# A hybrid decoder layer on one core: bias strips from a table of ready rows, and a new order of the projections and tasks

## The chip, the cores and the metric

The kernel runs on one core of a Trainium2 chip. A core has five engines that each work through their own list of instructions in order: TensorE (PE, matrix products), VectorE (DVE), ScalarE (ACT), GpSimd (POOL) and SyncE (SP), which here issues nearly all transfers. Engines wait for one another, and for transfers, at semaphores. The metric is the time of one execution on the device in microseconds (us); lower is better.

## The reference

One step of a decoder layer with D = 1024, for a prompt of 512 tokens and 8 sample tokens that continue cached sequences. One input projection gives the inputs of two mixers: gated linear attention with 4 heads (qa, ka, va, a gate of rank 16 called za, and an output gate ga), and dilated sliding-window attention with 8 heads of 64 (qb, kb, vb, gb). The second one matters here. Every query reads its keys at three patterns of distance (up to 128 in steps of 1, up to 512 in steps of 4, up to 2048 in steps of 16), each with a bias that depends on head and distance alone:

```
bias   = rel_bias[t5_bucket(dist)].T                    # one row per head
logits = einsum('bqhd,bqjhd->bhqj', q, k) * scale + bias
p      = exp(logits - m);   s = sum(p)                  # per pattern, merged by their sums
mix    = concat(o_a * silu(ga), o_b * silu(gb))
y      = mix @ w_out;  x_new = layer_norm(alpha * x + y, ln_g, ln_b)
```

All is in float32. Outputs are also the new recurrent states and the key and value rows.

## The kernel before

A float32 product is made as three passes over a high and a low part (`hi` times `hi`, `hi` times `lo`, `lo` times `hi`; helper `three`). The weights arrive as raw tiles (`raw_qb`, `raw_kb`, ...), a group of columns at a time; ACT casts the high part (`hi_kb<-raw_kb`), DVE subtracts to get the low part (`lo_kb`), and PE runs the group's 48 (256 feature columns: two token halves of 24) or 96 matmuls. These "dense" matmuls come in the order of the list `ORDER` (line 79).

All work is recorded by generators, each added as a task with a rank: `add(weight_loads(), 14.7)`, `add(strips(), 2.3)`. A planner (`class Plan`, line 201) simulates engines and transfers with costs of its own and at each moment begins, among what could start, the operation of the best rank; `dense()` has rank 100 and fills PE where nothing else is ready. What comes out is one fixed list of instructions for every engine, and the chip runs those lists whatever its real times are. So a changed rank or cost reorders all engines, SP's transfers too. Every recorded operation is emitted by line 377, so the profile shows that line nearly everywhere and groups must be told apart by tile names.

Transfers on SP go through eight semaphores in turn, so SP issues a transfer only when the one eight places earlier has landed. The order it issues them in is the order in which most of them land.

The bias goes this way. `bias_table()` makes `tsb`, for each of 8 heads a row of 768 values (512 by distance, 128 masked, 128 far ones), stores it to DRAM as `tab`, and a transfer inside DRAM copies it 35 times to `tabr` (280 rows of 768 values). `strips()` then loads for each head h and half pi a `strip` of 128 partitions: 256 values for the first half, and 64 more from a second transfer for the second half, both read from `tabr` at a shifted address in each partition. Three `st` buffers hold strips. `scores(m, pi)` makes products of queries and keys for two heads in banks `ps_s`; DVE multiplies these with the strip and sums (`pr<-ps_s,strip`), takes reciprocals (`ms`), scales, PE transposes (`ps_pt<-cf,pr`), and `ps_pv` takes the values in.

In names such as `strip70` the digits are head and half; `ps_s70` is the score bank of head 7 for that half, `ps_pt70` its transposition. `past` and `qbc` are the sample tokens' cached keys and broadcast queries, for POOL.

Of the kernel before, what the change touches and what calls it, by code (L numbers as in the profile page):

```python
# [11 lines left out]
F32 = mybir.dt.float32  # L12
# [42 lines left out]

T_N = 512
T_P = 768
T_R = 35
T_D = T_N + 128
T_W = T_D + 258  # L60

N_WARM = 7
ROWS = 66

SLOTS = dict(
    g=23,
    w=8, r=3,
    sv=4,
    pt=2, far=5, tp=2, vp=2,
    t2=2, st=3,  # L70
    pr=4,
    t1=5, ob=3,
    m=6)
BANKS = dict(d=3, s=3, t=2)


# [5 lines left out]
PIECE = 256  # L82
SPARE = 800.0

ORDER = "qa0 qb0 qb1 qb2 qb3 kb0 kb1 vb0 kb2 kb3 gb0 vb1 gb1 gb2 va0 gb3 va1 ga0 ga1 ga2 ga3".split()


class Op:
# [293 lines left out]
def trunk(ctx: ExitStack, tc: tile.TileContext, xT, xp, xs, state, ck, cv, w_in, wab, gnorm,  # L382
# [78 lines left out]
    o_pv, o_bs, o_as = cst("o_pv", [P, 4, NB]), vnt, cst("o_as", [P, NB * HA])  # L461
    yts = lt[:, 0, :].rearrange("p (m b) -> p m b", b=NB)
    ga_s, gb_s = cst("ga_s", [P, 4, NB]), cst("gb_s", [P, 4, NB])
    tabr = dram.tile([HB, T_R, T_P], F32, name="tabr")
    vad = dram.tile([NB, 512], F32, name="vad")
    qsd = dram.tile([NB, 512], F32, name="qsd")
    psd_s = dram.tile([64, 256], F32, name="psd_s")
# [103 lines left out]
    def first_loads():  # L571
        za = w_in[:, OFF["za"]:OFF["za"] + 16].rearrange("(k p) n -> p k n", p=P)
        for n, a, *b in FIRST:
            if n == "x":
                c = b[0] if b else slice(0, NT)
                if a % 2 == 0 and c.start == 0:
                    xraw.append((yield Need("g", f"x_raw{a}", [P, 2, NT])))
                yield D.dma_start(xraw[a // 2][:, a % 2, c], xT[a * P:(a + 1) * P, c])
            else:
                if a % 2 == 0:  # L580
                    ka_raw.append((yield Need("r", f"raw_ka{a}", [P, 2, W3])))
                rows = w_in[a * P:b[0] * P, P:P + W3]
                for q in (slice(0, P), slice(P, W3)) if a == 0 else (slice(0, W3),):
                    yield (S if a == 0 else D).dma_start(ka_raw[a // 2][:, a % 2:a % 2 + b[0] - a, q], rows.rearrange("(k p) n -> p k n", p=P)[:, :, q])
                if a == 0:
                    nc.scalar.preload_act_table_set("natural_log_exp_and_others")
            mark("first")
        yield D.dma_start(zw[:, :, 14:30], za)
        yield D.dma_start(wz, wab[None, 66:].to_broadcast([4, 32, 256]))
        mark("zw")  # L590
        yield D.dma_start(cf, c_f[:, :C_E2])
        add(weight_loads(), 14.7)
        B["rb_raw"] = yield Need("t1", "rb_raw", [64, NB, HB])
        for i in range(2):
            yield D.dma_start(B["rb_raw"][i * 32:i * 32 + 32], rel_bias[:, None, :].to_broadcast([32, NB, HB]))
        yield D.dma_start(cm_w, c_m)
        mark("const")
        yield D.dma_start(gn, gnorm)
        yield D.dma_start(same, c_f[:, C_MB:C_W])
# [93 lines left out]
    def token(g, evac_f, evac):  # L693

        for f in range(2):
            fs = slice(f * P, f * P + P)
            ps = yield bank("d", f"ps_{g.name}f{f}")
            for k in range(KT):
                yield g.at(k)
                h, l = xh[k][:, TS[0]], xl[k][:, TS[0]]  # L700
                yield from three(ps[:, :TW[0]], k, ((g.hi[k][:, fs], h), (g.hi[k][:, fs], l), (g.lo[k][:, fs], h)))
            add(evac_f(ps, f), 2)
        for t in (2, 3):
            ps = yield bank("d", f"ps_{g.name}{t}")
            ts = slice(NB + t * P, NB + t * P + P)
            for k in range(KT):
                yield from three(ps[:, :GW], k, ((xh[k][:, ts], g.hi[k]), (xh[k][:, ts], g.lo[k]), (xl[k][:, ts], g.hi[k])))
            add(evac(ps[:, :GW], t), 2)
        g.done(0)
        g.done(1)  # L710
# [165 lines left out]

    def bias_table():
        yield At("const")
        tab = dram.tile([HB, T_P], F32, name="tab")
        raw = yield Need("g", "ct_raw", [66, T_D])  # L880
        yield D.dma_start(raw, c_t[:, :T_D])
        ct = yield Need("g", "ct", [66, T_D], F32R)
        yield V.tensor_copy(ct, raw)
        free(raw)
        tsb = yield Need("g", "tsb", [HB, T_P])
        yield V.memset(tsb[:, T_N:T_P - P], NEG)
        yield At("rb")
        for c, to in ((slice(0, T_N), slice(0, T_N)), (slice(T_N, T_D), slice(T_P - P, T_P))):
            pt = yield bank("t", "ps_tab")
            yield T.matmul(pt[:HB, :c.stop - c.start], rb[:, 0, :], ct[:, c], start=True, stop=True)  # L890
            yield copy(tsb[:, to], pt[:HB, :c.stop - c.start])
            free(pt)
        yield D.dma_start(tab, tsb)
        free(ct, tsb)
        yield D.dma_start(tabr, tab[:, None, :].to_broadcast([HB, T_R, T_P]))
        mark("tab")


# [326 lines left out]
    def strips():  # L1225
        yield At("tab")
        yield At("qb", 1)
        for h0, pi in ((0, 0), (0, 1), (4, 0), (4, 1)):
            for h in range(h0, h0 + 4):
                yield At(f"kb{h // 2}{pi}")  # L1230
                strip = yield Need("st", f"strip{h}{pi}", [P, 256 + 64 * pi])
                plan.share(strip, 2)
                B["strip", h, pi] = strip
                row = tabr[h]
                yield D.dma_start(strip[:, 64 * pi:], bass.AP(tensor=row.tensor, offset=row.offset + T_N - P - 1, ap=[[T_P - 1, 4], [T_P - 4, 32], [1, 256]]))
                if pi:
                    yield D.dma_start(strip[:, :64], bass.AP(tensor=row.tensor, offset=row.offset + T_P - P + 31, ap=[[0, 4], [T_P - 1, 32], [1, 64]]))
                mark(f"strip{h}{pi}")

    def scores(m, pi):  # L1240
# [115 lines left out]
    def sample_queries():  # L1356
        yield At("qb", 8)
        yield from sample_rows(q_s, q_rows)
        yield D.dma_start(by_tile(qsd), q_rows)
        for bi in range(NB):  # L1360
            past = yield Need("sv", f"past{bi}", [P, 2, 512])
            yield D.dma_start(past, ck[bi])
            qbc = yield Need("t2", f"qbc{bi}", [P, 512])
            yield D.dma_start(qbc, qsd[bi:bi + 1, :].to_broadcast([P, 512]))
            add(sample_logit(bi, past, qbc), 17.8)

    def sample_logit(bi, past, qbc):
        for k in range(2):
# [346 lines left out]
    def out_unit(t, c, w, seeded=None):  # L1715
# [14 lines left out]
                for i, (l, r) in enumerate(((mh, hi), (mh, lo), (ml, hi))):  # L1730
                    yield T.matmul(ps, l, r, start=False, stop=k == KT - 1 and i == 2, skip_group_check=True)
        if seeded is not None:
            add(last_norm(t, ps), 2)
        elif w == GW + 2:
            add(early_mean(t, ps), 2)
        else:
            add(out_evac(t, c // GW, ps[:, :w]), 2)

    def out_first(*units):

# [4 lines left out]
            yield from out_half(g, f, ps[-1], range(4))  # L1745
        for (g, f), p in zip(units, ps):
            yield from out_half(g, f, p, range(4, KT))
            add(out_turn(g, f, p), 2)

    def out_half(g, f, ps, ks):  # L1750
        w, c = wo[g // 2], g % 2 * GW + f * P
# [92 lines left out]
    nc.vector.memset(warm, 0.0)  # L1844
    warm_ps = plan.alloc(bank("t", "warm_ps"))
    add(clear(), 0)
    add(first_loads(), 0)
    add(first_splits(), 1)
    add(fills(), 14.7)
    add(dense(), 100)  # L1850
# [1 line left out]
    add(gla_levels(), 20.3)  # L1852
    add(gla_diagonal(), 39.3)
    add(gla_state(), 14.3)
    add(gla_queries(), 24.3)
    add(strips(), 2.3)
    add(sample_queries(), 57.3)
    add(sample_softmax(), 10.7)
    add(sample_values(), 14.3)
    add(sample_v(vnt, "vnt", by_tile(vw_s)), 21.3)  # L1860
# [124 lines left out]
```

## Time and profile before

| | us |
|---|---|
| median of 3 runs | 275.88 (275.64 to 277.97) |
| profiled execution, span from first to last instruction | 275.6 |
| PE busy | 266.9 (97%) |
| DVE busy | 214.6 (78%) |
| ACT busy | 158.5 (58%) |
| last PE matmul ends at about | 266.3 |
| granted TensorE clock, mean | 0.996 |

The profiled execution itself took its span of 275.6 us by the profile; no other time of it is given. Times in the rows count from the first instruction. An entry in square brackets is idle time of the engine just before the row and what ended it. DVE and ACT have slack, PE almost none, so the questions to put to a row are when PE stands still, and what work of the other engines ends just before PE needs it.

### The profile page before, as it was taken

How to read it: one execution, taken by the hardware profiler on the slowest of the kernel's cores; microseconds unless marked ns; L12 is line 12 of the kernel's file. 1: busy time of each engine (PE TensorE's matmuls, PEld its weight loads, DVE VectorE, ACT ScalarE, POOL GpSimd, SP SyncE). 2: the span in 40 equal slices, each digit the busy share in tenths (PEclk: the TensorE clock that was granted, in tenths of full speed). 3: DMA queues.
4: the chain of work that ended last, by engine and by line, in shares of the span. 5: the costliest groups of instructions: out<-in, count | busy, mean ns of one | idle time of the engine just before them, and what ended most of it. 6: DMA issues, size and time to landing. Idle time of an engine off the chain costs nothing.

```text
span 275.6 us, 7460 instructions
## 1 busy us (share of the span) xinstructions
PE 266.9 (97%) x2881; PEld 252.1 (91%) x2881; DVE 214.6 (78%) x578; ACT 158.5 (58%) x478; POOL 52.8 (19%) x71
## 2 busy tenths in 40 slices
PE   8999999999899999999999999999999999999990
PEld 5999999999899989989999999999999999998890
DVE  4845899998989497998396963738999999239984
ACT  4727886475538583877686824535668886224401
POOL 3000000000534260703000633744242000000000
PEclk9999999999999999999999999999999999999998
DMA  7977939436967898556497979893897660980432
GB/s 219 340 181 190 266 91 235 125 104 179 311 188 161 243 291 276 157 115 157 87 258 195 221 202 188 250 279 92 265 246 194 179 223 6 293 239 0 180 129 76
DMA packets 61527, 52.58 MB, mean 191 GB/s; under 512 B 13645, under 2 KB 53715, under 8 KB 61493
## 3 DMA queue, kind: packets, MB, share of 16 engines
q1 hardware_dynamic: 60917, 51.66, 67.2%
q8 instruction: 22, 0.36, 0.5%
q10 hardware_dynamic: 576, 0.46, 0.5%
q14 instruction: 12, 0.10, 0.1%
HBM read 46.02 MB, written 6.42 MB: 190 GB/s over the span
## 4 chain that ended last, share of the span: by engine, by line
PE 94%; DVE 4%; ACT 1%; issue 0%; DVEq 0%
PE ps_ga L377 9%; PE ps_gb L377 9%; PE ps_qb L377 9%; PE ps_yf L377 8%; PE ps_kb L377 8%; PE ps_y L377 7%; PE ps_qa L377 5%; PE ps_ka L377 4%; PE ps_vb_f L377 4%; PE ps_va_f L377 4%; PE ps_vb L377 4%; PE ps_va L377 4%; PE ps_pv L377 3%; PE ps_s L377 3%; PE ps_pt L377 2%; PE ps_oa L377 2%
## 5 line engine op out<-in xcount | busy, mean ns | idle before, releaser
L377 POOL TENSOR_TENSOR past<-past,qbc 128x256 f32<-128x256 f32 x32 | 24.0, 782 | 99.5 <-DMA qbc<-qsd 91.6
L377 POOL TENSOR_TENSOR vv<-vv,pb 128x256 f32<-128x256 f32 x32 | 26.5, 860 | 55.3 <-DMA pb<-psd_s 49.4
L377 ACT ACTIVATE pr<-pr,ms 128x128 f32<-128x128 f32 (+3 forms) x48 | 22.8, 493 | 6.7 <-DVE ms L377 6.5
L377 DVE CUSTOM_DVE_ANT_0 pr<-ps_s,strip 128x128 f32<-128x128 f32 (+3 forms) x32 | 11.8, 410 | 6.9 <-PE ps_s L377 6.0
L377 ACT COPY pt<-ps_pt 128x256 f32<-128x256 f32 (+1 forms) x27 | 9.3, 354 | 11.1 <-PE ps_pt L377 11.1
L377 ACT ACTIVATE sg<-sg 128x264 f32<-128x264 f32 (+1 forms) x32 | 13.4, 420 | 0.5
L377 PE MATMUL ps_ka<-xx,hi_ka 128*128 128x264 f32 (+1 forms) x64 | 12.8, 296 | 0.0
L377 PE MATMUL ps_pt<-cf,pr 128*128 128x128 f32 x56 | 11.0, 274 | 0.0
L377 PEld LDWEIGHTS ps_ka<-xx,hi_ka 128*128 128x128 f32 x64 | 10.4, 201 | 0.0
L377 DVE TENSOR_REDUCE lt<-past 128x8 f32<-128x512 f32 x16 | 10.4, 671 | 0.0
L377 ACT ACTIVATE d<-d 128x512 f32<-128x512 f32 x11 | 6.9, 648 | 5.8 <-DVE d L377 5.8
L377 DVE TENSOR_REDUCE o_pv<-vv 128x4 f32<-128x1024 f32 x8 | 9.7, 1210 | 0.0
L377 ACT COPY feat_y<-ps_yf 128x256 f32<-128x256 f32 x7 | 2.6, 373 | 11.2 <-PE ps_yf L377 11.2
L377 PE MATMUL ps_ka<-xx,lo_ka 128*128 128x264 f32 (+1 forms) x32 | 9.0, 293 | 0.0
L377 DVE SCALAR_TENSOR_TENSOR y<-y,ps_yt 128x256 f32<-128x256 f32 x8 | 3.0, 418 | 6.9 <-PE ps_yt L377 6.9
L377 DVE SCALAR_TENSOR_TENSOR s<-v,ka_s,s 128x128 f32<-128x128 f32 x16 | 5.1, 343 | 3.2 <-DMA v<-vad 1.9
L377 PE MATMUL ps_qa<-xx,hi_ka 128*128 128x264 f32 (+1 forms) x32 | 7.4, 310 | 0.0
L377 PEld LDWEIGHTS ps_pt<-cf,pr 128*128 128x128 f32 x56 | 6.9, 140 | 0.3 <-issue 0.2
L377 PE MATMUL ps_kb<-xx,hi_kb__744 128*128 128x264 f32 (+1 forms) x32 | 6.2, 293 | 0.9 <-DVE ms L377 0.9
L377 PE MATMUL ps_pv<-pt,v 128*64 128x128 f32 (+1 forms) x80 | 6.9, 318 | 0.0
L377 PE MATMUL ps_gb<-xx,hi_gb__1903 128*128 128x264 f32 (+1 forms) x32 | 6.8, 295 | 0.0
L377 ACT CAST xx<-x_raw 128x520 fp32r<-128x520 f32 (+2 forms) x10 | 5.3, 539 | 2.6 <-DMA x_raw<-in_xT_dram 2.3
(570 smaller groups left out, 1065.8 us busy)
## 6 DMA issues: line engine op xcount, KB each, us to landing
past<-in_ck_dram SPq DMA_DIRECT2D x8, 512.0 KB
vv<-in_cv_dram SPq DMA_DIRECT2D x8, 512.0 KB
pb<-psd_s SPq DMA_DIRECT2D x16, 256.0 KB
s<-in_state_dram SPq DMA_DIRECT2D x4, 512.0 KB
strip<-tabr SPq DMA_DIRECT2D x16, 128.0 KB
qbc<-qsd SPq DMA_DIRECT2D x8, 256.0 KB
y<-in_xp_dram SPq DMA_DIRECT2D x4, 512.0 KB
x_raw<-in_xT_dram SPq DMA_DIRECT2D x6, 260.0 KB
```

Source lines behind the costliest of these rows:

```text
L377: getattr(eng.eng, op.fn)(*op.args, **op.kw)
```

## The change

There are two parts. First, the table. Instead of one row per head stored once and copied 35 times, `tab` receives each head's first 640 values four times at a pitch of 644, and `tabf` the 128 far values four times. Two transfers inside DRAM build from them `tabx`, 8 x 128 x 320: the row of every head and partition, ready for use (1024 rows of 256 values, and 1024 of 64). A strip is then one transfer with a plain address. Second, the order: in `ORDER` va0 goes ahead of gb2, and eleven tasks get other ranks. The planner's own estimates for transfers, and the number of buffers, stay (`SLOTS` is only written on one line).

```diff
-T_R = 35
+T_M = T_P - P
+T_R = T_M + 4
+T_S = 320
...
-ORDER = "... gb0 vb1 gb1 gb2 va0 gb3 va1 ga0 ga1 ga2 ga3".split()
+ORDER = "... gb0 vb1 gb1 va0 gb2 gb3 va1 ga0 ga1 ga2 ga3".split()
...
-    tabr = dram.tile([HB, T_R, T_P], F32, name="tabr")
+    tabx = dram.tile([HB, P, T_S], F32, name="tabx")
...
-        yield D.dma_start(tab, tsb)
+        yield D.dma_start(bass.AP(tensor=tab.tensor, offset=tab.offset, ap=[[4 * (T_R - 1), HB], [T_R, 4], [1, T_M]]),
+                          tsb[:, None, :T_M].to_broadcast([HB, 4, T_M]))
+        yield D.dma_start(tabf, tsb[:, None, T_M:].to_broadcast([HB, 4, P]))
...
-        yield D.dma_start(tabr, tab[:, None, :].to_broadcast([HB, T_R, T_P]))
+        for src, first, row, step, c, n in ((tab, T_N - P - 1, T_R - 1, -4, T_S - 256, 256), (tabf, 31, P, -1, 0, T_S - 256)):
+            yield D.dma_start(bass.AP(tensor=tabx.tensor, offset=tabx.offset + c, ap=[[32 * T_S, 4 * HB], [T_S, 32], [1, n]]),
+                              bass.AP(tensor=src.tensor, offset=src.offset + first, ap=[[row, 4 * HB], [step, 32], [1, n]]))
...
-                row = tabr[h]
-                yield D.dma_start(strip[:, 64 * pi:], bass.AP(tensor=row.tensor, offset=row.offset + T_N - P - 1, ap=[[T_P - 1, 4], [T_P - 4, 32], [1, 256]]))
-                if pi:
-                    yield D.dma_start(strip[:, :64], bass.AP(tensor=row.tensor, offset=row.offset + T_P - P + 31, ap=[[0, 4], [T_P - 1, 32], [1, 64]]))
+                yield D.dma_start(strip, tabx[h][:, T_S - 256 - 64 * pi:])
...
-            add(sample_logit(bi, past, qbc), 17.8)
+            add(sample_logit(bi, past, qbc), 20.3)
...
-    add(gla_queries(), 24.3)
+    add(gla_queries(), 18.5)
```

The other ranks: weight_loads 14.7 to 62.3, evac_f in `token` 2 to 61.9, last_norm 2 to 48.2, out_evac 2 to 7.4, out_turn 2 to 0.3, first_loads 0 to 3.9, sample_queries 57.3 to 21 (and sample_logit, gla_queries above).

Three places show what moves. On SP, where the table is built (`raw0_qb3`, `raw0_kb0` are raw weights), before:

```order
L377 DMA tab_283<-tsb_358 8x768 [waits DMAHW5_49,DVE_49,Activation_49]
L377 DMA raw0_qb2__436<-in_w_in_dram 128x8x128 [waits DMAHW6_49,DMAHW2_49,DVE_49]
L377 DMA tabr_91<-tab_283 280x1x768 [waits DMAHW7_49,DMAHW5_49]
L377 DMA raw0_qb3__472<-in_w_in_dram 128x8x128 [waits DMAHW3_49,DMAHW0_49,DVE_49]
L377 DMA raw0_kb0__496<-in_w_in_dram 128x8x128 [waits DMAHW4_49,DMAHW1_49,DVE_49]
L377 DMA raw0_kb1__531<-in_w_in_dram 128x8x128 [waits DMAHW6_49,DVE_49]
```

and now:

```order
L371 DMA tab_284<-tsb_357 8x4x640 [waits DMAHW5_49,DVE_49,Activation_49]
L371 DMA tabf_285<-tsb_357 32x1x128 [waits DMAHW6_49,DVE_49]
L371 DMA raw0_qb2__402<-in_w_in_dram 128x8x128 [waits DMAHW7_49,DMAHW2_49,DVE_49]
L371 DMA raw0_qb3__468<-in_w_in_dram 128x8x128 [waits DMAHW3_49,DMAHW0_49,DVE_49]
L371 DMA tabx_91<-tab_284 1024x1x256 [waits DMAHW5_49,DMAHW1_49]
L371 DMA tabx_91<-tabf_285 1024x1x64 [waits DMAHW6_49]
L371 DMA raw0_kb0__497<-in_w_in_dram 128x8x128 [waits DMAHW4_49,DVE_49]
L371 DMA raw0_kb1__537<-in_w_in_dram 128x8x128 [waits DMAHW7_49,DVE_49]
```

The weights qb3 went ahead of the table's copy, kb0 and kb1 stay behind it, and the copy is now two transfers.

On SP around the strip of head 7 (`raw1_va0` is half of va0's weights), before:

```order
L377 DMA cts_raw_2072<-in_c_t_dram 66x258 [waits DMAHW4_49,DVE_49,Activation_49]
L377 DMA out_4_dram<-kw1_1717 32x16x32 [waits DMAHW5_49]
L377 DMA qbc7_1947<-qsd_93 128x512 [waits DMAHW6_49,Pool_49]
L377 DMA strip70_2102<-tabr_91 128x1x256 [waits DMAHW7_49,DVE_49]
L377 DMA strip41_2118<-tabr_91 128x1x256 [waits DMAHW0_49,DVE_49]
L377 DMA strip41_2118<-tabr_91 128x1x64 [waits DMAHW1_49]
L377 DMA raw1_va0__2141<-in_w_in_dram 128x4x256 [waits DMAHW2_49,DVE_49]
```

and now, from the strips of heads 5 and 6 on:

```order
L371 DMA strip50_1869<-tabx_91 128x256 [waits DMAHW6_49,DVE_49]
L371 DMA strip60_1897<-tabx_91 128x256 [waits DMAHW7_49,DVE_49]
L371 DMA raw1_va0__1884<-in_w_in_dram 128x4x256 [waits DMAHW0_49,DVE_49,Activation_49]
L371 DMA qbc7_1866<-qsd_93 128x512 [waits DMAHW1_49,Pool_49]
L371 DMA sel_1948<-in_c_f_dram 66x224 [waits DMAHW2_49]
...
L371 DMA strip70_2040<-tabx_91 128x256 [waits DMAHW0_49,DVE_49]
L371 DMA strip41_2068<-tabx_91 128x320 [waits DMAHW1_49,DVE_49]
```

The half of va0's weights moved from behind strip70 to well ahead of it; the row left out stands for four small stores of key rows.

On PE, the scores that use strip60 and strip70, before:

```order
L377 MATMUL ps_vb1_f1_2107<-xx2_208,lo0_vb1__1585 128x264
L377 MATMUL ps_vb1_f1_2107<-xx2_208,hi0_vb1__1584 128x264
L377 MATMUL ps_s60_2114<-kp3_1756,qh1_733 128x128
L377 MATMUL ps_s70_2115<-kp3_1756,qh1_733 128x128 [waits DVE_49]
L377 MATMUL ps_s60_2114<-kp3_1756,qh1_733 128x128
```

and now:

```order
L371 MATMUL ps_gb0_1_2021<-xx6_302,hi0_gb0__1587 128x256
L371 MATMUL ps_gb0_1_2021<-xx6_303,hi0_gb0__1587 128x256
L371 MATMUL ps_s60_2071<-kp3_1774,qh1_737 128x128 [waits DVE_49]
L371 MATMUL ps_s70_2072<-kp3_1774,qh1_737 128x128 [waits DVE_49]
L371 MATMUL ps_s60_2071<-kp3_1774,qh1_737 128x128
```

These scores moved from inside vb1 to inside gb0, 35 dense matmuls earlier (754 dense matmuls stood ahead of them, now 719). PE has the same 2385 program matmuls in both lists, of which 1657 are dense. From the output projection on the lists are the same but for two transposition batches.

## Rows read from the trace of the kernel before

**Rows 1.** The page's first part: busy time, share of the span, instructions.

```profile
PE 266.9 (97%) x2881; PEld 252.1 (91%) x2881; DVE 214.6 (78%) x578; ACT 158.5 (58%) x478; POOL 52.8 (19%) x71
```

**Rows 2.** Busy time by stretch: length, PE, PEld, DVE, ACT, POOL, clock, DMA share, GB/s.

```profile
0.00:7.00 7.00, 5.81 (x20) 4.07 (x21) 2.98 (x16) 3.10 (x6) 2.29 (x7) 1.00 0.73 221
...
40.00:60.00 20.00, 20.00 (x300) 19.41 (x298) 19.91 (x41) 11.41 (x31) 0.00 (x0) 1.00 0.52 140
60.00:80.00 20.00, 19.05 (x387) 18.18 (x387) 18.08 (x45) 11.65 (x34) 6.14 (x8) 1.00 0.73 223
80.00:100.00 20.00, 20.00 (x205) 19.01 (x203) 15.51 (x44) 12.72 (x40) 8.60 (x12) 1.00 0.87 216
...
260.00:270.00 10.00, 9.08 (x63) 8.26 (x62) 8.70 (x28) 2.57 (x10) 0.00 (x0) 1.00 0.31 108
270.00:276.00 6.00, 0.00 (x0) 0.00 (x0) 2.31 (x6) 0.21 (x2) 0.00 (x0) 0.79 0.25 87
```

**Rows 3.** Timeline of PE around its stall: start, length, instruction, idle before.

```profile
73.09 0.41 PE L377 MATMUL ps_kb<-xx,hi_kb__744 128*128 128x264 f32 x2
73.33 0.28 PE L377 MATMUL ps_kb<-xx,lo_kb__745 128*128 128x264 f32 x1
74.57 0.50 PE L377 MATMUL ps_kb<-xx,hi_kb__744 128*128 128x256 f32 x2 [0.95 <-DVE ms L377]
```

**Rows 4.** Timeline of DVE there.

```profile
70.60 0.47 DVE L377 STREAM_TRANSPOSE kw<-ps_kb 128x256 f32<-128x256 f32 x1
...
74.33 0.20 DVE L377 RECIPROCAL ms<-ms 128x1 f32<-128x1 f32 x1
```

**Rows 5.** DMA queues from 66 to 72 us: packets, MB, share of 16 engines.

```profile
q1 hardware_dynamic: 808, 1.56, 93.0%
```

**Rows 6.** DMA queues from 72 to 77 us.

```profile
q8 instruction: 2, 0.03, 2.3%
```

**Rows 7.** Timeline of SP's queue while the table is built.

```profile
22.46 0.30 SPq L377 DMA_DIRECT2D tab<-tsb  x1
24.50 0.38 SPq L377 DMA_DIRECT2D raw_qb__436<-in_w_in_dram  x1
24.97 0.70 SPq L377 DMA_DIRECT2D tabr<-tab  x1
27.26 0.37 SPq L377 DMA_DIRECT2D raw_qb__472<-in_w_in_dram  x1
28.39 0.82 SPq L377 DMA_DIRECT2D raw_kb__496<-in_w_in_dram  x1
```

**Rows 8.** DMA from 24 to 37 us: all packets, and queue q1.

```profile
DMA packets 4422, 2.98 MB, mean 229 GB/s; under 512 B 72, under 2 KB 4139, under 8 KB 4419
...
q1 hardware_dynamic: 4419, 2.94, 78.9%
```

**Rows 9.** Timeline of ACT: the first use of kb0's weights.

```profile
40.51 1.03 ACT L377 CAST hi_kb__654<-raw_kb__496 128x1024 fp32r<-128x1024 f32 x1
```

**Rows 10.** The tile strip: its users, its loads, and who waited for it.

```profile
L377 DVE CUSTOM_DVE_ANT_0 pr<-ps_s,strip x32: 260/440/486, 71.0 to 148.7; 128x128 f32<-128x128 f32 x8, 128x256 f32<-128x256 f32 x8, 128x288 f32<-128x288 f32 x8, 128x320 f32<-128x320 f32 x8
L377 SPq DMA_DIRECT2D strip<-tabr x24: 507/556/1542, 64.7 to 139.7; - x24
...
  DMA strip<-tabr: 0.6, 1
```

**Rows 11.** Timeline of SP around strip70.

```profile
119.47 0.43 SPq L377 DMA_DIRECT2D qbc<-qsd  x1
120.25 1.92 SPq L377 DMA_DIRECT2D strip<-tabr  x3
122.90 0.41 SPq L377 DMA_DIRECT2D raw_va__2141<-in_w_in_dram  x1
```

**Rows 12.** Timeline of DVE: strip70's first use.

```profile
125.06 0.29 DVE L377 CUSTOM_DVE_ANT_0 pr<-ps_s,strip 128x128 f32<-128x128 f32 x1 [0.65 <-DMA strip<-tabr]
```

**Rows 13.** Timeline of PE: the scores of heads 6 and 7, and what follows.

```profile
122.08 0.44 PE L377 MATMUL ps_s<-kp,qh 64*128 64x128 f32 x4
...
123.30 1.52 PE L377 MATMUL ps_pv<-far,vp 128*64 128x256 f32 x16
124.65 1.58 PE L377 MATMUL ps_pv<-pt,v 128*64 128x128 f32 x18
```

**Rows 14.** DMA queues from 98 to 108 us.

```profile
q1 hardware_dynamic: 3163, 2.63, 92.0%
```

**Rows 15.** Timeline of PE: one change from dense work to scores.

```profile
107.34 0.28 PE L377 MATMUL ps_kb<-xx,lo_kb__1357 128*128 128x256 f32 x1
107.46 0.38 PE L377 MATMUL ps_pt<-cf,pr 128*128 128x128 f32 x2
107.77 0.50 PE L377 MATMUL ps_s<-kp,qh 64*128 64x256 f32 x4
```

**Rows 16.** The chain of waits at its end: start, length, engine, tile.

```profile
259.65 6.60 PE ps_y L377 x40
266.28 0.43 DVE y L377
...
271.98 0.40 DVE y L377
```

More of the change, by code (lines that the diff above doesn't have):

```diff
@@ L63 @@
 ROWS = 66
[L65 to L73, printed above, removed]
+SLOTS = dict(g=23, w=8, r=3, sv=4, pt=2, far=5, tp=2, vp=2, t2=2, st=3, pr=4, t1=5, ob=3, m=6)
 BANKS = dict(d=3, s=3, t=2)
@@ L83 @@
 SPARE = 800.0
-ORDER = "qa0 qb0 qb1 qb2 qb3 kb0 kb1 vb0 kb2 kb3 gb0 vb1 gb1 gb2 va0 gb3 va1 ga0 ga1 ga2 ga3".split()
+ORDER = "qa0 qb0 qb1 qb2 qb3 kb0 kb1 vb0 kb2 kb3 gb0 vb1 gb1 va0 gb2 gb3 va1 ga0 ga1 ga2 ga3".split()
 class Op:
@@ L591, in first_loads @@
         yield D.dma_start(cf, c_f[:, :C_E2])
-        add(weight_loads(), 14.7)
+        add(weight_loads(), 62.3)
         B["rb_raw"] = yield Need("t1", "rb_raw", [64, NB, HB])
@@ L701, in token @@
                 yield from three(ps[:, :TW[0]], k, ((g.hi[k][:, fs], h), (g.hi[k][:, fs], l), (g.lo[k][:, fs], h)))
-            add(evac_f(ps, f), 2)
+            add(evac_f(ps, f), 61.9)
         for t in (2, 3):
@@ L878, in bias_table @@
         yield At("const")
-        tab = dram.tile([HB, T_P], F32, name="tab")
+        tab = dram.tile([HB, 4 * (T_R - 1)], F32, name="tab")
+        tabf = dram.tile([HB, 4, P], F32, name="tabf")
         raw = yield Need("g", "ct_raw", [66, T_D])
@@ L1732, in out_unit @@
         if seeded is not None:
-            add(last_norm(t, ps), 2)
+            add(last_norm(t, ps), 48.2)
         elif w == GW + 2:
@@ L1736, in out_unit @@
         else:
-            add(out_evac(t, c // GW, ps[:, :w]), 2)
+            add(out_evac(t, c // GW, ps[:, :w]), 7.4)
     def out_first(*units):
@@ L1747, in out_first @@
             yield from out_half(g, f, p, range(4, KT))
-            add(out_turn(g, f, p), 2)
+            add(out_turn(g, f, p), 0.3)
     def out_half(g, f, ps, ks):
@@ L1846, in trunk @@
     add(clear(), 0)
-    add(first_loads(), 0)
+    add(first_loads(), 3.9)
     add(first_splits(), 1)
@@ L1854, in trunk @@
     add(gla_state(), 14.3)
-    add(gla_queries(), 24.3)
+    add(gla_queries(), 18.5)
     add(strips(), 2.3)
-    add(sample_queries(), 57.3)
+    add(sample_queries(), 21)
     add(sample_softmax(), 10.7)
```

## The prediction

> **What bounds the kernel now.** I read the page's first part, then busy time by stretch, then the chain of waits, and only then single places. PE is busy 266.9 us of a span of 275.6 [rows 1]. The stretches say where the other 8.7 us are [rows 2]. The first 7 us miss 1.19, the stretch from 260 on misses 0.92 and then all 6.00 (the span ends 0.4 before that window does), and between 7 and 260 one window alone is not full: 60 to 80 us, with 19.05 of 20. All other windows of 20 us, also those not shown, are full. The chain of waits agrees: PE's last matmul ends at about 266.3, and what follows is a chain of small steps on DVE and ACT and the last store [rows 16], 9.3 us to the end. So the time is PE's work, plus start and tail, plus one stall. The granted clock is 1.00 in every stretch until PE's work ends, so no part of the time waits for a higher one.
>
> The stall: a dense matmul of kb1's second half starts at 74.57 and the one before started at 73.33, where its like follow at 0.12 us (the pair at 73.09 and its successor at 73.33 are 0.24 apart) [rows 3]. That is 1.24 − 0.12 = 1.1 us. The row names DVE's `ms`. But the instruction that this matmul waits for in the program is the transposition `kw`, which ended at 71.07 [rows 4]; it had long been done, and the `ms` that ends at 74.53 has nothing to do with the bank. Something else held PE. From 66 to 72 us the ordinary transfers took 93.0% of all DMA engines and no row for PE's instruction queue appears there [rows 5]; it has 2 packets right after [rows 6], and the window has the densest instructions of all, 387 matmul records in 20 us [rows 2]. I read this as instructions that came late because data transfers filled the engines.
>
> **The change part by part, against the profiled span of 275.6** (the median 275.88 is 0.3 above; I add the 0.3 at the end).
>
> *PE's own work: 0.* The same 2385 matmuls, 1657 of them dense, run in both lists. What moves is which stands beside which. Changing from dense work to a batch of scores or transpositions costs something: after the last dense matmul at 107.34, two transpositions and the switch take until 107.77, 0.31 us behind the 0.12 of the dense one [rows 15]; two transpositions at about the dense cadence would be 0.24, so a switch is 0.07 us, and not over 0.19 if the second transposition were free. I count 50 such changes between dense and small work before and 49 or fewer in the new list, and three dense-to-small starts fewer at best: a gain from 0 to 3 × 0.19 = 0.6. I take 0.2, nearer the small price.
>
> *The eight strip transfers that go, and the plainer addresses: 0.* 24 issues become 16 at a median of 0.556 us each [rows 10], 4.4 us of SP's queue. SP is not on the chain, and DVE waited for a strip once in the whole run, 0.6 us [rows 10], a wait that did not reach PE, whose windows there are full. What hides it is PE's dense work; if that cover were gone, the gain would still be bounded by that 0.6.
>
> *The table built early: 0, bound 0 to +2.* `tabx` is 8 × 128 × 320 × 4 bytes = 1.31 MB, in place of 280 × 3072 = 0.86 MB. In that stretch 2.94 MB took 78.9% of 16 engines for 13 us, 56 ns per KB and engine [rows 8]; 0.45 MB more is 0.45 × 1000 × 56 / 16 ns = 1.6 us. The rows are smaller too: by packet instead, 1024 rows of 1 KB at 46.5 ns (3163 packets in 92.0% of 160 us of engines [rows 14]) and 1024 of 256 B at the 37 ns of a mean packet of rows 8 (78.9% of 208 us over 4419) come to 3.0 + 2.4 = 5.4 us, against 3.0 for `tabr` by bytes: 2.4 us more. One more issue adds at most 0.70 [rows 7], and the two stores `tab` and `tabf` instead of one 0.30. So raw kb0, which stays behind the table, comes 1.6 to 3.4 us later. When did it land before? From `raw_qb` at 24.50 up to and with kb0, 0.52 + 0.86 + 0.52 + 0.52 = 2.4 MB at 229 GB/s [rows 8] end at about 35.1, an estimate; ACT takes the tile at 40.51, without a wait [rows 9]. Slack 5.4, more than 3.4: nothing. qb3 is ahead of the table now, which can only help it. Would it fail, the cast of kb0 (1.03 us) would start late and PE's kb0 wait for the rest.
>
> [...] No run so far shows a row of 256 B alone.
>
> *Attention pulled forward: 0, bound 0 to +3.* The scores of several head pairs come earlier: those on strip60 and strip70 by 35 dense matmuls, 35 × 0.12 = 4.2 us. Nothing of PE is added, so it only matters whether what they need is there. The tightest is strip70: DVE waited 0.65 for it before [rows 12]. Its use now falls at 125.06 − 4.2 − 0.65 = 120.2 if DVE keeps pace. Its load was issued at 120.25 and came at 125.0, that is 4.8 us [rows 11, 12]. The load's buffer is set free earlier as well, by scores that moved 40 dense matmuls (4.8 us), so it could go at 115.5 and land at 120.2, just in time. But half of va0's weights and the last `qbc`, 0.52 + 0.26 = 0.78 MB, now stand ahead of it or closer to it in the queue; at 2.63 MB in 10 us [rows 14] that is 3.0 us. Not counted is what left the queue further up (gb1's and gb2's weights), which works the other way. DVE then waits 3 us at strip70, in order, with the low parts of gb1's weights queued behind. PE has to spare: after these scores come two `ps_pv` batches (about 2.9 us, from 123.30 to the end of the next [rows 13]) and 44 dense matmuls before the transposition `ps_pt70` needs the result, 44 × 0.12 + 2.9 = 8.2 us; of that the softmax of head 7 with reciprocal and scaling takes some 2 (0.3 and 0.4 for the two `pr`, four short steps, two scalings). Cover 6, wait 3: nothing.
>
> *The stall at 73 us: 0, bound −1.1 to 0.* PE's list up to kb1 and the first scores is the same, and the transfers of that stretch (`past`, `qbc`, four strips, vb1) are the same but for their order. I expect the same crowding and keep the stall.
>
> *Start and tail: 0.* The first matmuls and the lists from the output projection on are the same, so 1.2 at the start and 9.3 behind the last matmul stay. The new ranks of last_norm, out_evac and out_turn change nothing that PE waits for there.
>
> Sum: 275.6 − 0.2 + 0 = 275.4, and with the 0.3 between span and median some 275.7. The median's lowest run is 275.64; I put the forecast at **275.5**.
>
> **The rivals.**
>
> *Stall gone.* One refill a microsecond earlier is enough, and the new DMA order may do it: each strip with a second half is one request less, vb1's weights come behind one more `past`. Against: the engines were full for 6 us, not for one. It gives 275.5 − 1.1 = 274.4. [...]
>
> *Slower: strip70 late.* If the queue ahead of strip70 is fuller than reckoned, DVE waits there and PE comes to the end of its cover. It decides where the strip comes later than about 120.2 + 6 = 126 on the old clock. Up to 3 us more of queue, as for another 0.78 MB [rows 14], on the 3 reckoned reaches this point; PE loses beyond it whatever comes later, and all of DVE's queue behind it (the low parts of gb1, at 1.2 us each) follows. With 9 us of lateness in place of 3, it is 275.5 + 3 = 278.5 to 279. For: DVE did wait for that strip before. Against: the wait before was 0.65 and PE's windows stayed full.
>
> [...]
>
> *Faster by more.* Only if PE's cadence itself became better, for instance by a less loaded memory; no row suggests it.
>
> **How the numbers follow.** A measurement of this kernel tells 1%, 2.76 us, from no change: faster means below 273.1, slower above 278.6. Forecast (within 0.8 of 275.5): 0.53. Stall gone: 0.23, 274.4. kb0 late, or other small stalls under 2 us: 0.10, 276.5 to 277.5. strip70 late: 0.10, three quarters of it over the bound, and other stalls as large 0.02. Faster by more: 0.02, and 0.02 for a gain from two small things together. Chances: faster 0.04, within 1% 0.86, slower 0.10. The range takes the first three cases with the scatter of half a microsecond: 273.9 to 277.5; it leaves out 0.15 or so. The predicted time is the likeliest case's, 275.5.
>
> **What would show it.** Right: PE busy near 266.9 again, one window between 60 and 80 not full, 9.3 us behind the last matmul, `strip` loads 16 and DVE waiting on one or two of them for up to 3 us with PE's windows around 115 to 130 full. Stall gone: that window full, and the span 1.1 shorter. Strip late: a wait of PE on DVE at a `ps_pt` transposition or `ps_pv` near 125, above 1 us. kb0 late: ACT idle on DMA `raw_kb` ahead of 41. Wrong altogether: PE's busy time different from 266.9 by more than 1 us, which I have no mechanism for.

## The result: 0.4% slower

| | median, us | lowest to highest | runs |
|---|---|---|---|
| before | 276.56 | 275.41 to 277.97 | 16 |
| changed | 277.62 | 276.62 to 279.07 | 16 |

The ratio is 1.0044, 95% interval 1.0023 to 1.0065: slower by 0.6 to 1.8 us. (It is taken over all executions; the two medians alone stand at 1.0038.) The forecast was 275.5, a little below the old median, so the sign was wrong, and the time lies 0.1 us outside the range.

One thing has to be set right before two traces are compared. Every execution comes with its own span, and its time is 1.8 to 3.3 us above it, mostly about 2: the profiled execution of the changed kernel took 276.62 us with a span of 274.5. The span of 275.6 shown before thus belongs to an execution of about 277.7, one of the longest of that kernel, and not to one 0.3 below the median, as the prediction took it. The profile of the changed kernel is that of its shortest execution. So its span is 1.1 *shorter* than the one shown before, while the kernel is 1.1 *longer*: two single profiles of these kernels don't tell which is faster.

What a profile can show is where its own time went. The page's first part and the sum of its chain of waits by engine, after (PE busy 266.2 for 266.9 in [rows 1]):

```profile
PE 266.2 (97%) x2881; PEld 250.9 (91%) x2881; DVE 217.4 (79%) x577; ACT 158.8 (58%) x479; POOL 56.1 (20%) x71
...
PE 81%; DVE 10%; ACT 3%; DMA 2%; issue 2%; DVEq 0%; SPq 0%
```

Busy time by stretch after, columns as in [rows 2]:

```profile
0.00:7.00 7.00, 5.81 (x28) 4.07 (x28) 3.54 (x17) 3.33 (x7) 2.29 (x7) 1.00 0.75 220
...
60.00:80.00 20.00, 20.00 (x397) 19.21 (x397) 19.43 (x45) 11.62 (x34) 6.44 (x8) 1.00 0.76 229
80.00:100.00 20.00, 19.94 (x202) 18.63 (x201) 18.01 (x55) 13.48 (x42) 10.90 (x13) 1.00 0.87 243
...
220.00:240.00 20.00, 19.43 (x160) 19.14 (x160) 14.26 (x39) 9.01 (x24) 0.00 (x0) 1.00 0.53 128
260.00:270.00 10.00, 8.07 (x59) 7.45 (x57) 8.09 (x28) 1.45 (x5) 0.00 (x0) 1.00 0.14 56
```

The start misses the same 1.19 of busy time, but it is not the same start: 28 matmul records lie in it, where 20 lay before [rows 2]. The chains of the two profiles show the first real matmuls, before and then after:

```profile
5.02 1.37 PE ps_ka L377 x6
```

```profile
5.01 0.83 PE ps_ka L371 x6
```

Before, these six still start 0.22 us apart, about half the pace of the 0.12 that holds later. In the trace the record of a granted clock of 1.00 begins at 7.22 us before and at 5.07 after, and the starts go from 0.22 to 0.12 apart at these times; ahead of it nothing is recorded, and the view by stretch prints 1.00 all the same. In the second profiles of the two kernels, shown further down, it begins at 4.03 and 6.79. So this belongs to the execution and not to the kernel. PE's 101st matmul record starts at 16.70 before and at 15.82 after: 0.88 of the 1.1 us between the two spans lies ahead of it.

The stall between 60 and 80 [rows 3] is gone. A new hole of 0.57 stands between 220 and 240, where the old list was full. The timelines of PE and then DVE name it (columns as in [rows 3]):

```profile
220.83 0.63 PE L371 MATMUL ps_oat<-cf,oa 128*128 128x128 f32 x4
222.03 0.39 PE L371 MATMUL ps_yf<-mhb,hi_wo__3221 128*128 128x264 f32 x1 [0.57 <-DVE ga L371]
```

```profile
219.69 1.25 DVE L371 SCALAR_TENSOR_TENSOR ga<-ps_oat,gn,ga 128x128 f32<-128x128 f32 x4
...
220.96 0.69 DVE L371 TENSOR_TENSOR lo_wo__3735<-raw_wo__3566,hi_wo__3734 128x512 fp32r<-128x512 f32 x1
221.56 0.42 DVE L371 TENSOR_TENSOR ga<-ps_ga,sg 128x256 f32<-128x256 f32 x1
```

PE comes to a new bank of the output projection. That bank is the one of the last gate, and it is free only when DVE has multiplied the gate out (`ga<-ps_ga,sg`, 221.56 to 221.98). DVE did a subtraction of weights (`lo_wo`, 0.69) ahead of it. PE starts 0.05 behind its end.

The strips, their users and loads, after:

```profile
L371 DVE CUSTOM_DVE_ANT_0 pr<-ps_s,strip x32: 251/434/489, 70.4 to 151.3; 128x128 f32<-128x128 f32 x8, 128x256 f32<-128x256 f32 x8, 128x288 f32<-128x288 f32 x8, 128x320 f32<-128x320 f32 x8
L371 SPq DMA_DIRECT2D strip<-tabx x16: 338/384/1187, 64.6 to 130.6; - x16
```

16 issues at a median of 0.384 us in place of 24 at 0.556 [rows 10], and the line on waits for the strip's transfer is gone. The new weights of kb0 are cast at 42.07 without a wait on the transfer, and PE has no wait there:

```profile
42.07 1.04 ACT L371 CAST hi_kb__642<-raw_kb__497 128x1024 fp32r<-128x1024 f32 x1
```

The tail stayed: the chain's last row of PE ends at 265.24 and the span at 274.5, 9.3 us as before [rows 16]. (That row is not PE's last work. PE's last matmul ends at 269.1 before and 268.1 after, 6.5 and 6.4 us from the end; the chain had left PE by then.)

```profile
258.38 6.86 PE ps_y L371 x41
```

### The profile page after: what moved, and what is told of

Same layout as the page of the kernel before. It is cut to its first block, busy times and chain, and to the rows that moved or that the text cites. A ratio compares the mean times of both kernels' runs of the same rounds, so it can differ in the third digit from the quotient of the medians.

```text
span 274.5 us, 7452 instructions
## 1 busy us (share of the span) xinstructions
PE 266.2 (97%) x2881; PEld 250.9 (91%) x2881; DVE 217.4 (79%) x577; ACT 158.8 (58%) x479; POOL 56.1 (20%) x71
## 4 chain that ended last, share of the span: by engine, by line
PE 81%; DVE 10%; ACT 3%; DMA 2%; issue 2%; DVEq 0%; SPq 0%
PE ps_gb L371 9%; PE ps_qb L371 9%; PE ps_yf L371 8%; PE ps_y L371 7%; PE ps_kb L371 6%; PE ps_qa L371 4%; PE ps_va_f L371 4%; PE ps_ka L371 4%; PE ps_va L371 4%; PE ps_vb L371 3%; PE ps_pv L371 3%; PE ps_ga L371 3%; PE ps_s L371 3%; DMA strip<-tabx 2%; PE ps_pt L371 2%; PE ps_vb_f L371 2%
## 5 line engine op out<-in xcount | busy, mean ns | idle before, releaser
L371 POOL TENSOR_TENSOR past<-past,qbc 128x256 f32<-128x256 f32 x32 | 28.2, 913 | 86.5 <-DMA qbc<-qsd 79.0
L371 POOL TENSOR_TENSOR vv<-vv,pb 128x256 f32<-128x256 f32 x32 | 25.6, 831 | 64.3 <-DVE tp L371 28.0
L371 ACT ACTIVATE pr<-pr,ms 128x128 f32<-128x128 f32 (+3 forms) x52 | 24.5, 496 | 8.1 <-DVE ms L371 8.1
L371 ACT COPY pt<-ps_pt 128x256 f32<-128x256 f32 (+1 forms) x29 | 9.9, 350 | 6.8 <-PE ps_pt L371 6.8
L371 DVE TENSOR_TENSOR gb<-ps_gb,sg 128x256 f32<-128x256 f32 x8 | 3.4, 424 | 6.0 <-ACT sg L371 5.9
L371 ACT ACTIVATE qh<-ps_qb 128x128 fp32r<-128x128 f32 x16 | 5.2, 440 | 4.9 <-PE ps_qb L371 4.9
L371 DVE TENSOR_TENSOR xx<-x_raw,xx 128x520 fp32r<-128x520 f32 (+2 forms) x10 | 5.8, 589 | 1.7 <-ACT xx L371 1.6
```

The costliest lines, as they stand in the source:

```text
L371: getattr(eng.eng, op.fn)(*op.args, **op.kw)
```

## The experiments

All ratios are against executions of the kernel before on the same chip at the same time, with 95% intervals. Medians that were taken at different times are not compared with each other.

### The same kernels again

No edit: how far do profiles of one kernel differ?

> The kernel before once more, unaltered: ratio 1.000 by every theory. If the wait of 1.1 us at 73 us in the profile of before is a thing of single executions, it is absent here; if it belongs to the order of the work, it is here again with 0.9 to 1.3 us. The same for the length of the stretch at half cadence at the start (to 7.0 us before, to 5.9 in the profile of the change).

> The changed kernel once more, unaltered, to see its stretches in a second execution. Theory D (DVE's order): DVE and ACT need 22 to 23 us from the first batch of ps_oa to the first matmul of the output projection, so that PE waits there whenever it comes early; the wait at the first ps_yf is 0.3 to 1.5 us, the ratio to the kernel before 1.003 to 1.006. Theory T (table): PE's loss lies elsewhere, in the first 80 us or at a strip, and the wait at ps_yf is under 0.3 us or absent. Theory S (start only): ratio within 0.998 to 1.002.

Measured: before again 276.56, ratio 0.9988 [0.9964, 1.0013]; changed again 277.92, ratio 1.0033 [1.0009, 1.0057]. The loss repeats. The second profile of before has no stall at 73 us. It has a hole of 2.08 us elsewhere, in this window:

```profile
120.00:140.00 20.00, 17.92 (x194) 15.90 (x194) 14.49 (x54) 14.39 (x47) 2.81 (x4) 1.00 0.58 133
```

The strips' loads and who waited for them, second profile of before:

```profile
L377 SPq DMA_DIRECT2D strip<-tabr x24: 507/566/1527, 64.3 to 140.7; - x24
...
  DMA strip<-tabr: 4.5, 3
```

Its timelines of DVE and PE there, DVE's wait for strip70 and PE's wait behind it (ACT, idle 1.76 us until DVE's sums for that strip came, then reaches the copy `v` that PE's row names):

```profile
127.58 0.29 DVE L377 CUSTOM_DVE_ANT_0 pr<-ps_s,strip 128x128 f32<-128x128 f32 x1 [2.02 <-DMA strip<-tabr]
...
129.79 0.44 PE L377 MATMUL ps_pt<-cf,pr 128*128 128x128 f32 x2 [1.30 <-ACT v L377]
```

So the old strip loads do reach PE in some executions. The other 0.77 us of the hole stand at 121 us, behind DVE, which waited 1.75 us until 119.5 for a small table (`sel`); its load was issued right behind two strips that landed at 117.8 and 119.2. The first profile, where DVE waited 0.6 in all [rows 10], showed a harmless one. The second profile of the changed kernel again has the 0.57 at `ps_yf` and no wait for a strip. It also has a wait of 0.39, under 0.1 in the first, for ACT's exponentials:

```profile
87.02 0.33 PE L371 MATMUL ps_pt<-cf,pr 128*128 128x128 f32 x1 [0.39 <-ACT pr L371]
```

### Each half of the change through the planner

One kernel takes the table alone (old ranks and ORDER), one the ranks and ORDER alone (old table):

```
table_only:  before + tabx, bias_table(), strips() of the change
order_only:  before + ORDER "... gb1 va0 gb2 gb3 ...", the eleven ranks of the change
```

> The table of ready rows alone, with the projection order and all ranks of before (the planner still lays the lists out anew). Theory D: 0.999 to 1.001, no wait at the first ps_yf. Theory T: 1.003 to 1.006, the whole of the loss. Theory S: 1.000.

> The projection order and the eleven ranks alone, with the strips read from the replicated table as before. Theory D: 1.003 to 1.006 with a wait of PE on DVE at the first ps_yf. Theory T: 0.999 to 1.001. Theory S: 1.000.

Measured: 1.0415 [1.0377, 1.0454] and 1.0377 [1.0337, 1.0417], 10 to 12 us each; no expectation was near. Neither measures a half. The planner lays the whole list anew from the transfers and ranks it sees, and what came out for either half is a poor list. Busy time by stretch of the table alone:

```profile
200.00:220.00 20.00, 17.88 (x234) 16.83 (x220) 18.69 (x61) 16.58 (x73) 3.58 (x6) 1.00 0.86 228
220.00:240.00 20.00, 13.41 (x79) 12.46 (x80) 12.88 (x32) 6.76 (x16) 2.02 (x3) 0.66 0.47 124
```

Its waits of PE: what was waited for, us in total, times, longest:

```profile
PE ps_yf L371 <- ACT mhb L371: 5.9, 1, 5.9
PE ps_oat L371 <- DVE ga L371: 2.8, 1, 2.8
```

PE stands idle for 8.7 us between 200 and 240, far from any strip (the last load is issued at 137.9). The granted clock of the second window is 0.66, a mean over stretches at 1.00 and at 0.50: by the trace it is at 0.50 from 220.42, the end of the wait of 2.8, to 234.08, and PE's matmuls in that time start 0.22 apart in place of 0.12. With the order alone the longest wait is 4.4 us, at `ps_oat` near 223. To take the halves apart the lists have to be held fixed.

### Each half with the lists held fixed

The planner plans the one kind of transfer, and the other kind is issued in its places; the instructions of PE, DVE, ACT and POOL stay in the order of the one list.

```diff
+    def put(op, *instead):
+        op.instead = list(instead)
+        return op
-        getattr(eng.eng, op.fn)(*op.args, **op.kw)
+        for args in op.instead if op.instead is not None else [op.args]:
+            getattr(eng.eng, op.fn)(*args, **op.kw)
...
-                yield D.dma_start(strip[:, 64 * pi:], bass.AP(... ap=[[T_P - 1, 4], [T_P - 4, 32], [1, 256]]))
+                yield put(D.dma_start(strip[:, 64 * pi:], bass.AP(... ap=[[T_P - 1, 4], [T_P - 4, 32], [1, 256]])),
+                          (strip, tabx[h][:, T_S - 256 - 64 * pi:]))
```

> The planner lays out the lists as for the kernel before, with the old transfers; what is emitted in their places are the new ones (tab and tabf, the two copies into tabx, one load for each strip). PE, DVE, ACT and POOL lists are those of before, word for word; SP differs only in the table's and the strips' transfers. Theory D (the loss is in the new lists): 0.998 to 1.001, no wait of PE at the first matmuls of ps_yf. Theory T (the loss is in the table's transfers): 1.003 to 1.005.

> The reverse: the lists of the change, with the old table and the 24 strip loads emitted in the places of the new transfers. Theory D: 1.003 to 1.006 with the wait of 0.5 to 0.6 us at ps_yf on DVE ga. Theory T: 0.999 to 1.001.

> The new table under the lists of before once more, beside split_loads on the same chip: 0.996 to 0.999 if the gain of the first measurement (0.9978, interval 0.9956 to 1.0000) is one, and no DVE wait for a strip. If it was scatter: 0.999 to 1.001.

| | old lists | new lists |
|---|---|---|
| old table | 1 | 1.0067 [1.0032, 1.0101] |
| new table | 0.9978 [0.9956, 1.0000]; again 0.9973 [0.9952, 0.9993] | 1.0044 [1.0023, 1.0065] |

This is the decomposition. The table gains about 0.25%, 0.7 us, under the old lists, in two measurements (the interval of the first reaches 1). Under the new ones the difference 1.0067 − 1.0044 is of the same size, but the two intervals overlap, so there it is not shown. The lists cost 0.0067 × 276.7 = 1.9 us (by the interval 0.9 to 2.8). The net 1.2 us is the result. One expectation for the old table under the new lists failed: PE waits only 0.2 at `ps_yf` in its profile, and 0.7 at `ps_pt` near 127, with DVE waiting 2.7 for strips. The new table under the old lists is the kernel that beats both; its window from 120 to 140, and that from 220 to 240, are both full:

```profile
120.00:140.00 20.00, 20.00 (x217) 18.19 (x217) 14.83 (x52) 15.35 (x50) 3.89 (x4) 1.00 0.51 146
220.00:240.00 20.00, 20.00 (x169) 20.00 (x167) 14.43 (x40) 10.70 (x32) 0.00 (x0) 1.00 0.53 161
```

### What in the lists costs: single instructions held back

Under the new list and table one instruction is emitted later on its own engine, all else in place. First the `lo_wo` ahead of the last gate; then further ones that stood ahead of the softmax near 86 us.

```diff
+HOLD = {("DVE", "lo1_wo1", "raw1_wo1", 1): ("DVE", "ga1", "ps_ga3_1", 1)}   # last_gate_first
+  two_moves:   also ("DVE", "lt", "past1", 2) behind ("DVE", "pr30", "ps_s30", 2)
+  three_moves: first move, also ("ACT", "kd", "kd", 1) behind the pr30 exponentials
+               and ("ACT", "hi1_wo1", "raw1_wo1", 1) behind the two sg<-sg
```

> The changed kernel with one DVE instruction moved one place: the low part of w_out's piece 1 of columns 1 (first half, 0.6 us) stands behind, not ahead of, the product that reads the last gate bank ps_ga. All else is the same list. Theory D: PE's wait at ps_yf (0.57 in both profiles of the change) falls below 0.1 and the time by 0.5 to 0.6 us, so the ratio to before is 1.001 to 1.003. Rival: another wait takes its place within some us (the next transposition batch or mla), the time stays at 1.003 to 1.005.

> As last_gate_first, and the two reductions lt<-past1 stand behind the softmax sums of heads 2 and 3 instead of ahead of them (1.2 us of DVE), so that the transposition ps_pt at 85 to 87 us does not wait for ACT's pr (0.06 and 0.39 in the two profiles of the change). Theory D with this second place: both waits under 0.1, 0.999 to 1.002. If only the first place matters: as last_gate_first.

> The changed kernel with three instructions moved back a few places: on DVE the low part of w_out behind the last gate product (as in last_gate_first); on ACT the cast of that piece behind the two scalings sg of the last gate bank; on ACT the exponential kd<-kd (1.06 us) behind the four softmax exponentials of heads 2 and 3. Theory D: PE's waits at ps_pt near 86 us (0.06 to 0.60 in the profiles with the new lists) and at ps_yf (0.57) fall below 0.1 each, the time by 0.9 to 1.2 us against the change, ratio to before 0.997 to 1.000. Rival (the waits move on to the next consumer): 1.001 to 1.003.

Measured: 1.0010 [0.9987, 1.0033], 0.9999 [0.9977, 1.0020] and 1.0005 [0.9987, 1.0022]; the changed kernel stands at 1.0044 and 1.0033. The first move shortens PE's wait from 0.57 to 0.07. PE and DVE of last_gate_first at that place:

```profile
222.78 0.63 PE L343 MATMUL ps_oat<-cf,oa 128*128 128x128 f32 x4
223.48 0.39 PE L343 MATMUL ps_yf<-mhb,hi_wo__3221 128*128 128x264 f32 x1
```

```profile
223.00 0.42 DVE L343 TENSOR_TENSOR ga<-ps_ga,sg 128x256 f32<-128x256 f32 x1
```

The gate no longer has the subtraction ahead of it on DVE, and PE comes 0.06 behind its end. By time a gain of 0.23 to 0.34%, 0.6 to 0.9 us, goes with it, though the intervals overlap. The place near 86 did not yield: PE's wait for the softmax there was 0.06 and 0.39 in the two profiles of the changed kernel, 0.60 in last_gate_first, 0.33 with two moves, and with three it was 0.22 at the next transposition instead. Neither extra move is to be told from the first alone by time.

A third place, which no move touched, is in every profile of the new lists: PE halts near 55 us inside a batch of 32 small matmuls (`ps_og`). What PE waited for there, in the second profile of the changed kernel and in last_gate_first ("issue" is idle time for which the profile names nothing):

```profile
PE ps_og L371 <- issue: 0.3, 1, 0.3
```

```profile
PE ps_og L343 <- issue: 0.5, 1, 0.5
```

From its first matmul to the next work the batch takes 1.01 us in all seven profiles with the old lists. With the new ones it takes 1.39 and 1.74 (the changed kernel), 1.40 (old table), 1.95, 1.60 and 1.69 (one, two, three moves), a loss of 0.4 to 0.9. A packet on the instruction queue q8 begins 1.50, 1.37, 1.53, 1.00, 1.41 and 1.38 us ahead of the batch in these six: but for 0.01 us, the later it begins, the longer the halt. That points to instructions that come late at this place of the list. It was not tested, and with the old lists a packet begins 0.3 to 1.0 ahead of the batch and no halt follows.

So of the 1.9 us that the lists cost, the wait of 0.57 at the gate is shown and removed; 0.1 to 0.4 near 86 and 0.4 to 0.7 at `ps_og`, in the two profiles of the changed kernel, are seen and not removed. Together that is 1.0 and 1.7 us.

### What in the table gains: fewer transfers, or plainer addresses?

Three variants of the new table under the old lists. One loads a second-half strip in two transfers again (24 in all). One keeps 16 but leaves a hole behind each 32 rows, so that the source is 4 groups of 32 rows, as it was before. One keeps 128 rows but makes them 1284 bytes apart.

```diff
 split_loads:
-  (strip, tabx[h][:, T_S - 256 - 64 * pi:])
+  (strip[:, 64 * pi:], tabx[h][:, T_S - 256:])   and   (strip[:, :64], tabx[h][:, :64])
 four_groups:   T_G = 32 * T_S + 64
+  (strip, bass.AP(... ap=[[T_G, 4], [T_S, 32], [1, 256 + 64 * pi]]))
 odd_pitch:
-  tabx = dram.tile([HB, P, T_S])
+  tabx = dram.tile([HB, P, T_S + 1])
```

> The lists of before with the table of ready rows, but a strip of a second half is loaded in two transfers again (256 and 64 columns), so that SP has 24 strip transfers as before, all with plain addresses. Theory N (what helps is the number of transfers, since each holds one of eight places on SP and delays what stands behind it): DVE waits for strips again (0.6 to 4.5 us in all, as in the profiles with the old table), time 0.999 to 1.001. Theory A (what helps is the plain address): no wait for strips, 0.996 to 0.999 as with one transfer.

> The lists of before with the table of ready rows, one load for each strip; only the table's layout differs: behind every 32 rows stand 64 unused values, so that a load's address runs over 4 groups of 32 rows, as the skewed loads of before did, though each row stands plainly at a multiple of 256 bytes. Theory G (a strip load from the old table is slow since its address has 4 groups, whatever the rows' place): strips land late again, DVE waits for strips (over 0.5 us in all), SP's strip issues take 0.5 us at the median, time 0.999 to 1.001. Theory U (slow since the rows begin at odd places): no wait for strips, 0.996 to 0.999.

> The same with rows of 321 values in place of 320, so that a strip's 128 rows begin 1284 bytes apart at odd places, in one group with one pitch. Theory G: no wait for strips, issues of 0.32 to 0.4 us, 0.996 to 0.999. Theory U: DVE waits for strips, 0.999 to 1.001.

Measured: split_loads 0.9971 [0.9952, 0.9990], four_groups 0.9979 [0.9952, 1.0005], odd_pitch 0.9962 [0.9939, 0.9984]. Splitting loses nothing, so the number of transfers is not the gain. The other two don't part by time: four_groups' ratio lies where that of the plain table lies (0.9978), against the 0.999 to 1.001 of theory G, while its median, 276.79, equals that of before beside it, 276.78. Their profiles do part. Loads and waits of the strips with four groups:

```profile
L383 SPq DMA_DIRECT2D strip<-tabx x16: 509/549/1460, 64.0 to 138.5; - x16
...
  DMA strip<-tabx: 3.1, 2
```

PE's wait that follows, in the same kernel's timeline:

```profile
128.20 0.44 PE L383 MATMUL ps_pt<-cf,pr 128*128 128x128 f32 x2 [1.26 <-ACT v L383]
```

The same with the odd pitch, where no wait on a strip is listed:

```profile
L382 SPq DMA_DIRECT2D strip<-tabx x16: 319/406/739, 66.0 to 138.2; - x16
...
```

From the semaphore events of the traces, worked out for three strips that were issued one after another and for issue to landing of single ones (us):

```
                      three landings                 strip50, strip60, strip70: issue to landing
before                78.55, 81.10, 82.66            5.47, 6.31, 4.67     source in 4 groups
four_groups           78.07, 80.21, 82.03            7.04, 7.89, 6.28     source in 4 groups
new_table_old_lists   77.91, 78.27, 78.71            2.39, 2.87, 2.18     source of 128 rows
odd_pitch             80.03, 80.39, 80.83            2.10, 2.80, 2.14     source of 128 rows
```

1.6 to 2.6 us apart with four groups, 0.4 with 128 rows, though the packets of 1 KB have the same median of 46 ns in all of them. So in these runs the strip lands late by the form of its address, a source whose slowest dimension has 4 entries: with the rows in plain places as well (6.28 to 7.89 for the three single loads of four_groups), and with 128 rows not even at odd places (2.10 to 2.80 in odd_pitch). The events also count it. A load of 128 rows raises its semaphore in 16 steps, all of them 1.6 us or more behind the issue. A load with 4 groups, in all five profiles that have such loads, raises it in 5: one ahead of the rest (0.9 to 3.4 us behind the issue), then 4 late ones, the last of them the landing. And 128 packets of 46 ns are 1.5 us on 4 engines and 0.4 on 16, an estimate that meets the spacings. So that the old strips ran on 4 engines is an estimate from the packets' 46 ns, the spacing of the landings (2 us for 4 groups against 0.4) and the 4 late steps against 16. The traces used here don't name a packet's engine, and it was not tried with other numbers of groups.

That this is also what gains the time is less firm, since the times don't part. One count sets the scatter of the start aside: from PE's 101st matmul record to the end, the profiles with the old lists take 258.9 and 259.7 with the old table, 259.4 with four groups, and 257.0 to 258.1 with 128 rows (four profiles). The changed kernel takes 258.7 and 259.4.

## Why the prediction was wrong

**"Attention pulled forward: 0" and "Start and tail: 0" failed.** The first looked for the tightest place at strip70 and asked whether that strip would be late. Under the new lists it was not late in any profile with the new table. What was late are places that neither step looked at. The last gate's bank at 222 us, 0.57, lost its slack to one `lo_wo` on DVE; the prediction took the lists from the output projection on as the same, and said that the new ranks there "change nothing that PE waits for there". (Which of the eleven ranks put the subtraction ahead of the gate was not tried.) The others are the softmax near 86, 0.06 and 0.39, and the halt at `ps_og` near 55, 0.4 and 0.7. The lists cost 1.9 us where 0 stood, and of that only the gate's wait is shown by an experiment.

**"The eight strip transfers that go, and the plainer addresses: 0" failed too, the other way.** It was bounded by the 0.6 that DVE waited in one profile [rows 10]. In the next profile of the same kernel it waited 4.5, and PE 1.3 behind it. The rival "strip70 late" priced a real mechanism, with its place and chain (strip70, DVE, then PE at `ps_pt` near 125 to 130), but as one that the change brings. It belongs to the kernel before, and the new table takes it away: 0.7 us on average under the old lists. That the old source runs over 4 groups stood in the code, and the step did not ask what it does to a load.

**The stall at 73 us: kept, and wrong as a forecast.** It is absent in the second profile of before and in all five profiles of the old lists with the new table and its variants, so it is a thing of one execution and not of the old list. The rival "stall gone" drew 1.1 us from the median for an event that the median hardly holds. The reading as late instructions was not tested, but the traces speak for it: the packet on q8 that begins at 72.07 here, 1.3 us ahead of the last matmul before the stall, begins between 68.8 and 70.6 in the six profiles without one. Why it was late is open.

**The reference failed.** To add "the 0.3 between span and median" set times against a span that they are 2 us above. The sum of changes against 275.6 then compared an execution that had a stall with a median of executions mostly without. As the sum was near 0 the forecast stayed near the old median, and the three runs shown had a lower median (275.88) than all sixteen (276.56). Of the miss of 2.1 us (277.62 − 275.5), 0.7 is this, 1.1 is the change itself, and 0.4 the small gain that was forecast.

**Readings that were wrong.** That "no part of the time waits for a higher one" (a higher clock) overlooks the start. There matmuls begin 0.22 us apart in place of 0.12, in the first profiles of before and of the change, until the record of a granted clock of 1.00 begins; that is between 4.0 and 7.2 us in the fifteen profiles, and the 101st matmul record starts between 15.8 and 16.8, so single executions part by up to a microsecond. The last matmul of PE does not end at 266.3 but at 269.1. The chances of the cases add up to 1.02. No run shows the loss of the case with kb0 late (276.5 to 277.5): in the profile of the changed kernel the packets of 256 B have a median of 18 ns, by which 1024 of them are 1.15 us on 16 engines, an estimate, where 2.4 was reckoned, and the cast of kb0 at 42.07 did not wait for its transfer.

**What held.** PE's work is the same. The losses at the switches between dense and small work, summed from the starts of PE's matmuls, fell by 0.5 to 0.7 us, by what is counted as dense, where 0.2 stood and 0.6 was the bound. The table built early cost nothing at kb0. The chain's tail is 9.3 again.

**Signs that were named.** 16 strip loads, and 9.3 behind the chain's last matmul: seen. DVE waiting up to 3 us on strips: not with the new table. The window from 60 to 80 not full: not seen.

## What to carry to other kernels

A list that a planner lays out has no parts that stay as they were: compare each engine's order at every place where PE takes over a bank, above all near the end, where DVE's extra work is spent. To measure half of a change whose other half sets the order, plan one kind and issue the other in its place; undoing it through the planner measured the planner (4%, for halves worth −0.25% and +0.7%). Look at the form of a load's address: here strip50, strip60 and strip70 landed 2.1 to 2.9 us behind their issue where the source's slowest dimension was the 128 partitions, and 4.7 to 7.9 where it was 4 groups. And look at several profiles before a wait is priced, since one shows which waits exist in that execution. Before two spans are compared, take off what differs at their start.

## What the runs showed that was not expected

- Two profiles of one kernel put their loss in different places: first 1.1 us at 73 and nothing near 130, then nothing at 73 and 2.1 in two pieces at 121 and 130. The times scatter with them, from 275.3 to 278.0 for the kernel before in one set, and from 274.9 to 277.4 for its new-table version beside it.
- The record of a granted clock of 1.00 began between 4.0 and 7.2 us in the fifteen profiles, whatever the kernel, and the 101st matmul record with it between 15.8 and 16.8.
- SP needs longer to issue a strip whose source has 4 groups: a median of 0.549 to 0.566 us, against 0.358 to 0.426 with 128 rows.
- Rows 1284 bytes apart landed as fast as rows 1280 apart (three strips 0.36 and 0.44 apart in both), and 1024 rows of 256 bytes in the table's second transfer did not delay kb0 (cast at 42.07 without a wait on its transfer).
- In the two kernels in which PE stood idle longest its granted clock fell to 0.50: for 13.7 us with the table alone (0.66 as the mean from 220 to 240), from the end of a wait of 2.8 us and through one of 5.9, and twice for 3.4 us with the order alone (0.91 as the mean from 60 to 80 and from 220 to 240), behind waits of 1.3 and 4.4. With the wait of 1.3 in the second profile of before it stayed at 1.00 (the mean from 120 to 140), and four_groups, which has one as long, shows 0.993 over the whole execution, against 0.969 and 0.984 in these two.
